# Hybrid decoder layer: issuing background work by per-tile readiness estimates, at finer points

## The chip, the cores and the metric

The kernel runs on one core of a Trainium2 chip. The metric is the device time of one execution in microseconds (us). Before the change three runs took 1051.8, 1048.09 and 1047.04 us; the median is 1048.09 us.

## The reference, cut to what matters

One layer of a decoder on 512 tokens of width 1024: a token-mixing part with two branches, cross-attention into 256 memory tokens, and a mixture of 32 experts. All data are fp32.

```python
h = rms_norm(x, norm_mix_g);  proj = h @ w_in                     # 1024 -> 5120
c_a, c_g, q_r, f_r, i_r, g_r, gate_c, gate_r = split(proj)
# branch 1: u = c_a*sigmoid(c_g); causal depthwise convolution, 31 taps, 512 channels
u = silu(layer_norm(conv(u) + b, ln_g, ln_b));  y_conv = u @ conv_w_out
# branch 2 (HGRN2, 4 heads): decayed scores from cumsum(log f), state per 128 tokens
y_rec = (rms_norm(hgrn2(q_r, f_r, i_r)) * silu(g_r)) @ hgrn_w_out
x = x + (sigmoid(gate_c)*y_conv + sigmoid(gate_r)*y_rec) @ w_mix_out
x = x + cross_attention(rms_norm(x), rms_norm(mem))               # xa_w_q, k, v, o
x = rms_norm(x + moe(rms_norm(x)))     # top group, top 2 of 8 experts in it; 3 matrices each
```

## The kernel before

**Foreground.** The dense products run one after another on TensorE. Each fp32 weight piece of 128 x 1024 is loaded by SyncE into `raw`, rounded to `wh` on ScalarE and the rest `wl = raw - wh` is formed on GpSimd (for the first 16 pieces every second one on VectorE); `push_split` does this (L161 to L171). Each k-step of a product is three matmuls, high x high, high x low and low x high (`mm3`, L226). `gemm_t` (L233) makes transposed outputs, 256 columns at a time in two PSUM banks: one weight piece (`chunk`) serves 24 matmuls, and three pieces are split ahead. `gemm_n` (L261) makes outputs with tokens on partitions. The order of the products is: keys, values (memory); then from `w_in` the HGRN values, f, q, the conv pairs, g, the two gates; then `hgrn_w_out` (`ev_rec`), `conv_w_out` (`ev_conv`), `w_mix_out`, cross-attention, router, experts.

**Background.** Everything else of the mixing part is written as Python generators, "threads": `prepare` (norm of x, transposes, constants), `hgrn_scores` and `hgrn_state` (Ln, scan, seven levels of `z` with Exp on ScalarE and score matmuls `psc` on TensorE, then the states `po`, `pk`, `pst`, then `pot`, `gT`, `oh`, `ol`), `conv` (120 tap instructions on VectorE into two PSUM banks `cva`, then the layer norm: `pmu`, `pvar`, and the split into `chl`). All of this is decided when the program is built: `pump` (L196) is called between groups of foreground matmuls and runs the threads' next steps into the instruction streams. Every engine takes its stream in order, so where a step stands in the stream decides what it holds up.

**The planner.** `Meter` (L43) adds an estimated cost to a clock per engine for each instruction issued. `pump` lifts VectorE's and ScalarE's clocks to TensorE's, then runs a thread while VectorE is less than `SLACK` (3000 ns) ahead of TensorE and the time that the thread last yielded (its due time) has come on TensorE's clock. A bare `yield` is due at once; `now()` is the later of VectorE's and ScalarE's clocks. Before the change an engine's clock does not wait for another engine's results, GpSimd costs nothing, and `gemm_t` calls `pump` twice in each weight piece, after 12 matmuls each. Where a thread's result is needed, `drain` runs the rest of it at once: `drain(t_sc)` at L858 ahead of the `hgrn_w_out` product and `drain()` at L866 ahead of the `conv_w_out` product.

All engine calls go through `Meter.call`, so almost every instruction has line L55; the tile names tell them apart.

**After the mixing part** the expert weights (192 pieces of 1 MB) are loaded into the 16 large buffers of the pool (tag `u`) as these come free, in a fixed order.

Of the kernel before, what the change touches and what calls it, by code (L numbers as in the profile page):

```python
# [19 lines left out]
PSUM = bass.MemoryType.PSUM  # L20
# [8 lines left out]
NH = 4  # L29
# [13 lines left out]
class Meter:  # L43


    def __init__(self, engine, cost):
        self.engine, self.cost, self.clock = engine, cost, 0.0

    def __getattr__(self, name):
        f = getattr(self.engine, name)  # L50

        def call(*args, **kw):
            out = args[0] if args else kw["out"]
            self.clock += self.cost(out, kw)
            return f(*args, **kw)  # L55

        return call
# [10 lines left out]
def act_cost(out, kw):  # L68
    return 200 + 0.72 * free_size(out)


def no_cost(out, kw):
    return 0


def pe_cost(out, kw):
    n = free_size(out)
    if kw.get("lhsT") is not None and kw["lhsT"].dtype == F32R:
        return 0.42 * n if n >= 256 else 213
    return 1.68 * n if kw.get("lhsT") is not None else 110  # L80
# [3 lines left out]
def tile_layer(ctx, tc, x, mem, norm_mix_g, w_in, conv_w, conv_b, conv_ln_g, conv_ln_b, conv_w_out,  # L84
# [5 lines left out]
    meters = [Meter(e, c) for e, c in ((nc.vector, dve_cost), (nc.scalar, act_cost), (nc.gpsimd, no_cost),  # L90
                                       (nc.tensor, pe_cost))]
    V, S, G, PE = meters
# [69 lines left out]
    def push_split(lo_eng=None):  # L162
# [7 lines left out]
        (lo_eng or (V if i < WIDE and i % 2 else G)).tensor_tensor(out=lo, in0=raw, in1=hi.bitcast(F32), op=OP.subtract)  # L170
# [25 lines left out]
    def pump():  # L196
        t0 = meters[3].clock
        for m in meters[:2]:
# [34 lines left out]
    def gemm_t(ncols, nk, act, n, evac, parts=1, mid=None):  # L233
        for c in range(0, ncols, 256):
            pss = [bank("pt") for _ in range(2)]
            ws = []
            for kh in range(nk // 4):
                ws.append(chunk(SPL if parts == 1 else 2))
                for f in range(2):
                    if parts == 1:  # L240
                        for kk in range(4):
                            k = kh * 4 + kk
                            mm3(pss[f][:, :n], [t[:, kk, f * 128:(f + 1) * 128] for t in ws[kh]], act(k),
                                k == 0, k == nk - 1)
                        if kh == nk // 4 - 1:
# [356 lines left out]
    def hgrn_state():  # L602
# [5 lines left out]
        for b in range(NB):  # L608
# [7 lines left out]
            if b < NB - 1:  # L616
# [5 lines left out]
                yield now()  # L622
# [6 lines left out]
                else:  # L629
                    for h in range(NH):  # L630
                        V.scalar_tensor_tensor(hs[:, h, :], hs[:, h, :], elast[:, h * 4 + b:h * 4 + b + 1],
                                               pst[:, h * 128:(h + 1) * 128], op0=OP.mult, op1=OP.add)
            S.copy(out=oN[:, b, :], in_=po)
            yield now()
# [14 lines left out]
        for h in range(NH):  # L649
# [3 lines left out]
            V.scalar_tensor_tensor(gT[:, h, :], ps, vec("on", 0), gT[:, h, :], op0=OP.mult, op1=OP.mult)  # L653
            S.activation(ohl[0][:, h, :], gT[:, h, :], AF.Copy, scale=0.5)
            V.scalar_tensor_tensor(ohl[1][:, h, :], gT[:, h, :], 0.5, ohl[0][:, h, :].bitcast(F32),
                                   op0=OP.mult, op1=OP.subtract)
            yield

    def hgrn_scores():

        S.activation(cum, cum, AF.Ln)
        yield
        ck = u4("ck")
        S.activation(ck, kT, AF.Ln, bias=tiny)
# [5 lines left out]
        ST = u4("ST")  # L670
        state["ST"] = ST
        G.memset(ST, 0.0)

# [47 lines left out]
        for li, m in enumerate(LEVELS):  # L721
# [4 lines left out]
            V.tensor_tensor(out=zv[:, :, 1, :], in0=cv[:, :, 1, :], in1=mid, op=OP.subtract)  # L726
            S.activation(z, z, AF.Exp)
            yield
            if prev is None:
                yield from until("q")  # L730
            else:
                yield from top_scores(prev, 2 * m, at) if li < 3 else scores(li - 1, prev, prev, at)
            V.tensor_tensor(out=zv[:, :, 1, :], in0=zv[:, :, 1, :], in1=qv[:, :, 1, :], op=OP.mult)
            at = now() + (1500 if li else 3000)
# [6 lines left out]
        S.activation(qe, cum, AF.Exp)  # L741
        elast = const.tile([128, 16], F32, name="elast")
# [4 lines left out]
        V.tensor_tensor(out=kevb, in0=cvb[:, :, 127:128].to_broadcast([128, 16, 128]), in1=ckb, op=OP.subtract)  # L747
        S.activation(ke, ke, AF.Exp)
        yield from scores(6, prev, prev, at)
        V.tensor_copy(out=elast, in_=qe.rearrange("p c (n t) -> p (c n) t", t=128)[:, :, 127])  # L750
# [16 lines left out]
    def conv():  # L767
# [9 lines left out]
        for c2 in (0, 2):  # L777
# [12 lines left out]
            if c2 == 0:  # L790
                cv = u4("cv")
                chl.extend((u4("ch", F32R), u4("cl", F32R)))
            for c in (c2, c2 + 1):
# [3 lines left out]
        yield now() + 1000  # L797
        pmu = col_sum(chl, "pmu")
        mu = q4("mu")[:, :512]
        S.activation(mu, pmu, AF.Copy, scale=1.0 / CW)  # L800
        sq = u4("sq")
        for c in range(5):
            if c < 4:
                V.tensor_tensor(out=cv[:, c, :], in0=cv[:, c, :], in1=mu, op=OP.subtract)
# [1040 lines left out]
```

## Time and profile before

| | before |
|---|---|
| median of three runs | 1048.09 us |
| profiled execution, its own time | 1050.78 us |
| its span | 1049.0 us |
| TensorE busy | 965.0 us (92%) |
| VectorE busy | 484.6 us (46%) |
| ScalarE busy | 283.2 us (27%) |
| GpSimd busy | 232.5 us (22%) |
| DMA, read from memory | 258.21 MB, 250 GB/s over the span |

The profile shows one execution. An instruction's row has its start and its duration in us; matmuls are pipelined and their ends are modelled, so two matmuls that follow each other overlap in their rows, and the distance between starts tells what one costs. "Idle before" in square brackets is the time for which the engine stood, and what ended it. PE is TensorE, DVE VectorE, ACT ScalarE, POOL GpSimd. PEclk is the granted share of TensorE's full clock in a stretch.

### The profile page before, as it was taken

The numbers are of one execution on the slowest core, as the hardware profiler recorded it, in microseconds if no ns is written. First come the engines' busy times: TensorE is split into PE (matmuls) and PEld (weight loads), VectorE is DVE, ScalarE is ACT, GpSimd is POOL, SyncE is SP. The second block draws the span as 40 slices with busy tenths as digits, with TensorE's granted clock in tenths as the row PEclk, the third lists the DMA queues.
The fourth block names the chain that finished last, engine by engine and source line by source line (L and its number), as shares of the span: only waits on it lengthen the run. The fifth ranks groups of instructions, "written<-read, shape, count | busy, mean of one in ns | idle before, by whom it ended". The sixth has DMA issues, their size and how long they took to land.

```text
span 1049.0 us, 13180 instructions
## 1 busy us (share of the span) xinstructions
PE 965.0 (92%) x4951; PEld 630.5 (60%) x4951; DVE 484.6 (46%) x967; ACT 283.2 (27%) x461; POOL 232.5 (22%) x122
## 2 busy tenths in 40 slices
PE   7999999998999999999999999999979999776674
PEld 7888778886788888888875444444325543221221
DVE  5581469778985661553335233333303552110113
ACT  5543543432433433354321111111101110000003
POOL 3354321331442575433220000000000000000001
PEclk9999999999999999999999999999989999899988
DMA  9433221111322333212878999999999999999994
GB/s 339 166 87 101 62 80 42 61 61 61 100 87 75 101 108 112 81 61 97 348 283 315 356 371 414 417 417 417 419 416 421 418 417 416 418 417 419 415 397 153
DMA packets 80671, 260.81 MB, mean 249 GB/s; under 512 B 8475, under 2 KB 39356, under 8 KB 59996
## 3 DMA queue, kind: packets, MB, share of 16 engines
q1 hardware_dynamic: 75194, 252.81, 62.4%
q0 software_dynamic: 1728, 3.80, 0.9%
q10 hardware_dynamic: 3682, 3.32, 0.9%
q8 instruction: 40, 0.66, 0.3%
q14 instruction: 27, 0.22, 0.1%
HBM read 258.21 MB, written 4.19 MB: 250 GB/s over the span
## 4 chain that ended last, share of the span: by engine, by line
PE 65%; DMA 23%; issue 4%; DVE 4%; ACT 2%; POOL 1%; SPq 0%; POOLq 0%; DVEq 0%; ACTq 0%
PE pt L55 25%; PE pn L55 12%; PE pg L55 10%; DMA wd<-in_moe_w_down_dram 8%; DMA wg<-in_moe_w_gate_dram 7%; DMA wu<-in_moe_w_up_dram 7%; PE py L55 5%; PE psc L55 3%; PE pc L55 3%; DVE z L55 2%; PE pd L55 1%; PE px L55 1%; PE pot L55 1%; POOL wl L55 1%; PE pw L55 1%
## 5 line engine op out<-in xcount | busy, mean ns | idle before, releaser
L55 POOL TENSOR_TENSOR wl<-raw,wh 128x1024 fp32r<-128x1024 f32 x79 | 195.1, 2474 | 319.0 <-ACT wh L55 303.8
L55 PE MATMUL py<-wd,sghd 128*32 128x512 f32 (+2 forms) x512 | 113.4, 625 | 18.8 <-DMA wd<-in_moe_w_down_dram 18.5
L55 PE MATMUL pt<-hh,wh 128*128 128x512 f32 x288 | 115.6, 401 | 5.0 <-DVE gT L55 3.7
L55 ACT CAST wh<-raw 128x1024 fp32r<-128x1024 f32 x88 | 91.9, 1049 | 100.0 <-PE pt L55 42.5
L55 PE MATMUL pt<-hh,wl 128*128 128x512 f32 x288 | 114.4, 397 | 3.4 <-POOL wl L55 3.4
L55 PE MATMUL pg<-wg,XT 128*32 128x512 f32 (+2 forms) x512 | 103.8, 609 | 14.5 <-DMA wg<-in_moe_w_gate_dram 14.3
L55 PE MATMUL pt<-hl,wh 128*128 128x512 f32 x288 | 114.1, 396 | 0.0
L55 PE MATMUL pg<-wu,XT 128*32 128x512 f32 (+2 forms) x512 | 104.7, 630 | 9.2 <-DMA wu<-in_moe_w_up_dram 9.2
L55 DVE TENSOR_TENSOR xs<-pc,xs 128x512 f32<-128x512 f32 x96 | 58.5, 680 | 88.9 <-PE pc L55 88.9
L55 POOL DMA_INDIRECT X<-xd,idx x12 | 12.1, 1007 | 344.7 <-DVE idx L55 173.6
L55 PEld LDWEIGHTS py<-wd,sghd 128*32 128x32 f32 (+2 forms) x512 | 31.5, 130 | 91.4 <-issue 52.2
L55 DVE SCALAR_TENSOR_TENSOR yl<-py,wsl,yh 128x512 fp32r<-128x512 f32 x26 | 19.4, 750 | 133.4 <-ACT yh L55 132.1
L55 PEld LDWEIGHTS pg<-wg,XT 128*32 128x32 f32 (+2 forms) x512 | 31.3, 129 | 82.7 <-issue 57.6
L55 DVE SCALAR_TENSOR_TENSOR cva<-uT,ca,cva 128x482 f32<-128x482 f32 (+29 forms) x120 | 77.8, 728 | 0.0
L55 PEld LDWEIGHTS pg<-wu,XT 128*32 128x32 f32 (+2 forms) x512 | 30.8, 132 | 75.4 <-issue 53.3
L55 PEld LDWEIGHTS pt<-hh,wh 128*128 128x128 f32 x288 | 55.1, 191 | 17.4 <-DVE gT L55 4.0
L55 PEld LDWEIGHTS pt<-hh,wl 128*128 128x128 f32 x288 | 55.2, 192 | 16.1 <-POOL wl L55 4.3
L55 PEld LDWEIGHTS pt<-hl,wh 128*128 128x128 f32 x288 | 55.3, 192 | 11.3
L55 ACT COPY sghd<-ph 128x512 f32<-128x512 f32 x13 | 7.6, 585 | 161.5 <-PE ph L55 161.5
L55 DVE SCALAR_TENSOR_TENSOR sghd<-pg,wsl,sghd 128x512 f32<-128x512 f32 x13 | 9.8, 750 | 86.3 <-PE pg L55 73.4
L55 ACT ACTIVATE yh<-py,wsl 128x512 fp32r<-128x512 f32 x26 | 17.9, 687 | 114.6 <-PE py L55 114.3
L55 PE MATMUL pt<-h,wh 128*128 128x512 f32 (+1 forms) x160 | 41.5, 348 | 0.0
(324 smaller groups left out, 1563.4 us busy)
## 6 DMA issues: line engine op xcount, KB each, us to landing
wg<-in_moe_w_gate_dram SPq DMA_DIRECT2D x57, 1024.0 KB
wd<-in_moe_w_down_dram SPq DMA_DIRECT2D x56, 1024.0 KB
wu<-in_moe_w_up_dram SPq DMA_DIRECT2D x52, 1024.0 KB
raw<-in_w_in_dram SPq DMA_DIRECT2D x40, 512.0 KB
wu<-in_moe_w_up_dram SPq DMA_DIRECT2D x24, 512.0 KB
wd<-in_moe_w_down_dram SPq DMA_DIRECT2D x16, 512.0 KB
wg<-in_moe_w_gate_dram SPq DMA_DIRECT2D x14, 512.0 KB
raw<-in_xa_w_v_dram SPq DMA_DIRECT2D x4, 1024.0 KB
```

Of the source, the lines that this page charges most:

```text
L55: return f(*args, **kw)
```

## The change

1. **The planner's estimates.** A call now starts at the latest of its engine's clock and the estimated times at which the tiles that it reads are written (`Meter.ready`, by tile, 60 ns after the writer's end). A large all-SBUF `tensor_tensor` on VectorE or GpSimd is put behind an overlapping one of the other engine (`Meter.port`). ScalarE's and TensorE's costs are changed (a matmul of 512 columns from 215 to 227 ns, an fp32 one of 128 columns from 215 to 111 ns, 80 ns for a change of type), GpSimd gets costs, and `pump` lifts its clock too.
2. **Finer points.** `gemm_t` calls `pump` after every three matmuls.
3. **Due times.** In the threads, ScalarE instructions that read a VectorE result are put behind a `yield` of VectorE's clock (before `Exp` of `z`, `ke`, before the splits of the convolution, between `gT` and `oh`), TensorE's steps behind other offsets. `Ln` is cut into eight pieces with a `yield` after each pair, and the clearing of `ST` goes ahead of it.
4. **The convolution's norm** is regrouped: four subtractions first, then squares and splits; the last loop has five rounds in place of six.
5. **Low parts in halves.** GpSimd forms `wl` in two instructions of 512 columns.

No arithmetic is added or removed.

```diff
@@ -43,6 +43,9 @@ class Meter
+    ready, port = {}, []
     def __init__(self, engine, cost):
@@ -51,7 +54,19 @@ Meter.call
             out = args[0] if args else kw["out"]
-            self.clock += self.cost(out, kw)
+            aps = [a for a in list(args) + list(kw.values()) if hasattr(a, "tensor")]
+            t = max([self.clock] + [Meter.ready.get(a.name, 0) for a in aps if a is not out])
+            c = self.cost(out, kw)
+            if name == "tensor_tensor" and c > 300 and all(a.space == SB for a in aps):
+                for t0, t1, e in Meter.port[-4:]:
+                    if e is not self and t0 <= t < t1:
+                        t = t1
+                Meter.port.append((t, t + c, self))
+            self.clock = t + c
+            for a in (out, kw.get("accum_out")):
+                if a is not None:
+                    Meter.ready[a.name] = self.clock + 60
             return f(*args, **kw)
@@ -66,18 +81,20 @@ cost functions
 def act_cost(out, kw):
-    return 200 + 0.72 * free_size(out)
-def no_cost(out, kw):
-    return 0
-def pe_cost(out, kw):
+    return 200 + 0.77 * free_size(out) + (190 if kw.get("accum_out") is not None else 0)
+def pool_cost(out, kw):
+    return 130 + 2.22 * free_size(out)
+def pe_cost(out, kw, last=[None]):
     n = free_size(out)
-    if kw.get("lhsT") is not None and kw["lhsT"].dtype == F32R:
-        return 0.42 * n if n >= 256 else 213
-    return 1.68 * n if kw.get("lhsT") is not None else 110
+    r = kw.get("lhsT") is not None and kw["lhsT"].dtype == F32R
+    c = 80 if r != last[0] else 0
+    last[0] = r
+    return c + (0.4425 * n if r else max(0.87 * n if kw.get("lhsT") is not None else 0, 110))
@@ -87,8 +104,9 @@ tile_layer
     nc = tc.nc
-    meters = [Meter(e, c) for e, c in ((nc.vector, dve_cost), (nc.scalar, act_cost), (nc.gpsimd, no_cost),
+    meters = [Meter(e, c) for e, c in ((nc.vector, dve_cost), (nc.scalar, act_cost), (nc.gpsimd, pool_cost),
                                        (nc.tensor, pe_cost))]
+    Meter.ready, Meter.port = {}, []
     V, S, G, PE = meters
@@ -167,7 +185,10 @@ push_split
         S.copy(out=hi, in_=raw)
-        (lo_eng or (V if i < WIDE and i % 2 else G)).tensor_tensor(out=lo, in0=raw, in1=hi.bitcast(F32), op=OP.subtract)
+        e = lo_eng or (V if i < WIDE and i % 2 else G)
+        for c in (0, 512) if e is G else (0,):
+            sl = slice(c, c + 512 if e is G else 1024)
+            e.tensor_tensor(out=lo[:, sl], in0=raw[:, sl], in1=hi[:, sl].bitcast(F32), op=OP.subtract)
         splits.append(tuple(t.rearrange("p (k c) -> p k c", k=nk) for t in (hi, lo)))
@@ -195,7 +216,7 @@ pump
         t0 = meters[3].clock
-        for m in meters[:2]:
+        for m in meters[:3]:
             m.clock = max(m.clock, t0)
@@ -242,6 +263,8 @@ gemm_t
                                 k == 0, k == nk - 1)
+                            if kk < 3:
+                                pump()
                         if kh == nk // 4 - 1:
@@ -619,7 +642,7 @@ hgrn_state
                 S.copy(out=kn, in_=pk)
-                yield now()
+                yield S.clock + 1500
                 pst = bank("pst")
@@ -630,8 +653,9 @@ hgrn_state
                                                pst[:, h * 128:(h + 1) * 128], op0=OP.mult, op1=OP.add)
+            yield meters[3].clock + 1000
             S.copy(out=oN[:, b, :], in_=po)
-            yield now()
+            yield
             for h in range(NH):
@@ -651,25 +675,27 @@ hgrn_state
             V.scalar_tensor_tensor(gT[:, h, :], ps, vec("on", 0), gT[:, h, :], op0=OP.mult, op1=OP.mult)
+            yield V.clock
             S.activation(ohl[0][:, h, :], gT[:, h, :], AF.Copy, scale=0.5)
...
                                    op0=OP.mult, op1=OP.subtract)
-            yield
+            yield V.clock
-        S.activation(cum, cum, AF.Ln)
-        yield
+        ST = u4("ST")
+        state["ST"] = ST
+        G.memset(ST, 0.0)
         ck = u4("ck")
-        S.activation(ck, kT, AF.Ln, bias=tiny)
+        for h in range(NH):
+            S.activation(cum[:, h, :], cum[:, h, :], AF.Ln)
+            S.activation(ck[:, h, :], kT[:, h, :], AF.Ln, bias=tiny)
+            yield S.clock
         for h in range(NH):
...
         yield
-        ST = u4("ST")
-        state["ST"] = ST
-        G.memset(ST, 0.0)
@@ -724,14 +750,17 @@ hgrn_scores
             V.tensor_tensor(out=zv[:, :, 1, :], in0=cv[:, :, 1, :], in1=mid, op=OP.subtract)
+            yield V.clock
             S.activation(z, z, AF.Exp)
+            ez = S.clock
             yield
...
                 yield from top_scores(prev, 2 * m, at) if li < 3 else scores(li - 1, prev, prev, at)
+            yield ez
             V.tensor_tensor(out=zv[:, :, 1, :], in0=zv[:, :, 1, :], in1=qv[:, :, 1, :], op=OP.mult)
-            at = now() + (1500 if li else 3000)
+            at = V.clock + 2500
             yield
@@ -739,14 +768,17 @@ hgrn_scores
         S.activation(qe, cum, AF.Exp)
+        eq = S.clock
         elast = const.tile([128, 16], F32, name="elast")
...
         V.tensor_tensor(out=kevb, in0=cvb[:, :, 127:128].to_broadcast([128, 16, 128]), in1=ckb, op=OP.subtract)
+        yield V.clock
         S.activation(ke, ke, AF.Exp)
         yield from scores(6, prev, prev, at)
+        yield eq
         V.tensor_copy(out=elast, in_=qe.rearrange("p c (n t) -> p (c n) t", t=128)[:, :, 127])
@@ -790,23 +822,24 @@ conv
                 chl.extend((u4("ch", F32R), u4("cl", F32R)))
+            yield V.clock
             for c in (c2, c2 + 1):
...
                 yield
-        yield now() + 1000
+        yield V.clock + 1000
         pmu = col_sum(chl, "pmu")
+        yield PE.clock + 300
         mu = q4("mu")[:, :512]
...
         sq = u4("sq")
-        for c in range(5):
-            if c < 4:
-                V.tensor_tensor(out=cv[:, c, :], in0=cv[:, c, :], in1=mu, op=OP.subtract)
-                S.activation(sq[:, c, :], cv[:, c, :], AF.Square)
-            if c:
-                split(sq[:, c - 1, :], c - 1)
-            yield
-        yield now() + 4000
+        for c in range(4):
+            V.tensor_tensor(out=cv[:, c, :], in0=cv[:, c, :], in1=mu, op=OP.subtract)
+        for c in range(4):
+            yield Meter.ready[cv.name] - 750 * (3 - c) if c < 3 else V.clock
+            S.activation(sq[:, c, :], cv[:, c, :], AF.Square)
+            split(sq[:, c, :], c)
+        yield V.clock + 500
         pvar = col_sum(chl, "pvar")
@@ -815,18 +848,21 @@ conv
         yield from rsqrt_steps(v, y, t)
-        for c in range(6):
+        for c in range(5):
             if c < 4:
...
                 V.tensor_scalar(cv[:, c, :], cv[:, c, :], hv[:, c:c + 1], hv[:, 4 + c:5 + c], op0=OP.mult, op1=OP.add)
+                w = V.clock
+            if c:
+                V.scalar_tensor_tensor(cv[:, c - 1, :], sq[:, c - 1, :], 1.0, cv[:, c - 1, :], op0=OP.add, op1=OP.mult)
+            yield w
+            if c < 4:
                 S.activation(sq[:, c, :], cv[:, c, :], AF.Tanh)
-            if 0 < c < 5:
-                V.scalar_tensor_tensor(cv[:, c - 1, :], sq[:, c - 1, :], 1.0, cv[:, c - 1, :], op0=OP.add, op1=OP.mult)
+            if c:
+                yield V.clock
                 S.copy(out=chl[0][:, c - 1, :], in_=cv[:, c - 1, :])
-            if c > 1:
-                V.tensor_tensor(out=chl[1][:, c - 2, :], in0=cv[:, c - 2, :], in1=chl[0][:, c - 2, :].bitcast(F32), op=OP.subtract)
-            yield
+                V.tensor_tensor(out=chl[1][:, c - 1, :], in0=cv[:, c - 1, :], in1=chl[0][:, c - 1, :].bitcast(F32), op=OP.subtract)
         dump("cs", cv)
```

## Rows read from the trace of the kernel before

**Rows 1.** Page, part 4: the chain that ended last, shares of the span by engine

```profile
PE 65%; DMA 23%; issue 4%; DVE 4%; ACT 2%; POOL 1%; SPq 0%; POOLq 0%; DVEq 0%; ACTq 0%
```

**Rows 2.** Busy time in stretches: start:end, length, engines' busy us, PEclk, DMA share, GB/s

```profile
25.00:30.00 5.00, 5.00 (x44) 5.00 (x43) 1.99 (x3) 2.09 (x2) 1.23 (x2) 1.00 0.84 318
...
160.00:313.00 153.00, 144.06 (x740) 121.56 (x740) 132.74 (x189) 56.35 (x93) 51.67 (x21) 0.98 0.22 69
500.00:650.00 150.00, 146.87 (x738) 86.88 (x737) 55.41 (x204) 31.71 (x66) 17.50 (x9) 1.00 0.89 345
650.00:1025.00 375.00, 328.33 (x1654) 132.88 (x1653) 105.02 (x258) 34.68 (x54) 8.89 (x9) 0.96 1.02 416
```

**Rows 3.** Waits of TensorE, 10 to 560 us: total us, times, longest us

```profile
PE pt L55 <- DVE gT L55: 3.7, 1, 3.7
PE pt L55 <- POOL wl L55: 3.4, 2, 1.7
...
PE psc L55 <- DVE z L55: 2.7, 3, 1.1
...
PE px L55 <- DVE xn L55: 1.9, 1, 1.9
PE pst L55 <- ACT kn L55: 1.4, 2, 0.7
PE pt L55 <- ACT wh L55: 1.3, 2, 0.8
```

**Rows 4.** First and last of four 5 us stretches with lower PEclk, columns as rows 2

```profile
45.00:50.00 5.00, 4.15 (x15) 3.60 (x16) 4.43 (x5) 1.20 (x3) 0.00 (x0) 0.66 0.00 0
...
275.00:280.00 5.00, 5.00 (x16) 3.97 (x15) 5.00 (x9) 1.05 (x1) 2.42 (x2) 0.67 0.67 209
```

**Rows 5.** Timeline around 125 us, engine by engine: start, us, instruction, [idle before]

```profile
122.13 1.92 ACT L55 ACTIVATE z<-z 128x2048 f32<-128x2048 f32 x1 [6.23 <-DVE z L55]
123.95 1.03 ACT L55 CAST wh<-raw 128x1024 fp32r<-128x1024 f32 x1
...
123.61 0.39 PE L55 MATMUL pt<-hl,wh 128*128 128x512 f32 x1
123.84 0.39 PE L55 MATMUL pt<-hh,wl 128*128 128x512 f32 x1
125.03 0.50 PE L55 MATMUL pt<-hh,wh 128*128 128x512 f32 x1 [0.81 <-ACT wh L55]
...
127.48 0.50 PE L55 MATMUL pt<-hh,wl 128*128 128x512 f32 x1 [1.72 <-POOL wl L55]
```

**Rows 6.** Timeline of VectorE at 42 us and at 250 us

```profile
42.39 3.40 DVE L55 SCALAR_TENSOR_TENSOR xn<-xs,st,gmix 128x1024 f32<-128x1024 f32 x1
...
249.55 0.68 DVE L55 SCALAR_TENSOR_TENSOR gT<-gT,pt 128x512 f32<-128x512 f32 x1
```

**Rows 7.** Timeline of ScalarE: first square of x, Ln and table loads, convolution's splits

```profile
35.28 1.06 ACT L55 ACTIVATE sq<-xs 128x1024 f32<-128x1024 f32 x1
...
109.49 1.28 ACT L55 ACT_TABLE_LOAD   x1
110.79 1.92 ACT L55 ACTIVATE cum<-cum 128x2048 f32<-128x2048 f32 x1
...
267.46 0.59 ACT L55 CAST ch<-cva 128x512 fp32r<-128x512 f32 x1 [3.43 <-DVE cva L55]
```

**Rows 8.** GpSimd's low parts by tile: ns min/median/max, first and last start

```profile
L55 POOL TENSOR_TENSOR ml<-gate,mh x8: 1284/1515/1747, 372.2 to 393.0; 128x512 fp32r<-128x512 f32 x8
...
L55 POOL TENSOR_TENSOR wl<-raw,wh x79: 2355/2397/3440, 13.6 to 536.9; 128x1024 fp32r<-128x1024 f32 x79
```

**Rows 9.** Timeline of VectorE: last write of `ol`, last write of `chl`, last `ev_rec`

```profile
262.14 0.69 DVE L55 SCALAR_TENSOR_TENSOR ol<-gT,oh 128x512 fp32r<-128x512 f32 x1 [0.70 <-ACT oh L55]
...
352.10 1.45 DVE L55 TENSOR_TENSOR cl<-cv,ch 128x512 fp32r<-128x512 f32 x2
...
367.30 0.69 DVE L55 SCALAR_TENSOR_TENSOR gate<-gate,pt 128x512 f32<-128x512 f32 x1 [2.04 <-PE pt L55]
```

More of the change, by code (lines that the diff above doesn't have):

```diff
@@ L19 @@
 AX = mybir.AxisListType
-PSUM = bass.MemoryType.PSUM
+PSUM, SB = bass.MemoryType.PSUM, bass.MemoryType.SB
 SP, ACT, DVE = mybir.EngineType.SP, mybir.EngineType.Activation, mybir.EngineType.DVE
```

## The prediction

> **What bounds the kernel now.** I first read the chain that ended last: it runs through TensorE for 65% of the span, through DMA for 23%, and through the other engines for 7% together [rows 1]. Then the stretches [rows 2]. From 650 to 1025 us the DMA engines are full at 416 GB/s, so there the weights set the pace. From 500 to 650 us they move 345 GB/s: a load starts when a buffer comes free, and TensorE's progress frees it. So the kernel is two parts in series: up to about 560 us TensorE's stream sets the pace, then a stream of weights whose start hangs on that stream. The change touches only the first part. What TensorE gains there comes off the end one for one, unless a new wait takes it; nothing in the second part waits for a fixed time.
>
> TensorE's busy share is no guide to what is left in the first part, since modelled ends hide gaps of a quarter microsecond. Two views tell it. The waits of TensorE [rows 3]: six groups, 14.4 us in 11 waits. And the granted clock: four stretches of 5 us, each right behind a wait for `xn`, `wl`, `gT` or `wl`, stand at 0.66 to 0.67 of the full 2.4 GHz, a mixture of the two levels of 1.2 and 2.4 GHz [rows 4]; the engine stood before each of them and was at full clock up to the wait. A stretch at 0.66 does 3.3 us of work in 5 us, so each costs 1.7 us, 6.7 us in all. A listed wait is also short by the overlap: starts are 0.23 us apart in the undisturbed stream (123.61 to 123.84), and from 123.84 to 125.03 it lost 1.19 - 0.23 = 0.96 us where 0.81 is listed [rows 5]; 0.15 x 11 = 1.7 us more. Sum: 14.4 + 6.7 + 1.7 = 22.8 us. This is the most that a better order can take from TensorE's stream, since its matmuls stay the same.
>
> **Why these waits are there.** At 125 us the order is at fault, not the work. `Exp` of `z` stands on ScalarE for 6.23 us for VectorE's `z`; behind it in the stream stands a rounding `wh`, which starts at 123.95; `wl` follows on GpSimd, and the matmuls stand 0.81 and 1.72 us [rows 5]. At 272 us it is the same with the convolution's split `ch`, which stood 3.43 us for the taps [rows 7]. At 250 us VectorE is late: its `gT` for a product's bank starts at 249.55 and the matmul that needs the bank at 250.29 [rows 3, 6]. At 45 us the product `xn` took 3.40 us on VectorE, beside a low part on GpSimd, and the transposes stood for it [rows 3, 6].
>
> **The change part by part**, each place with its wait, its 0.15 us a time and its clock:
>
> (a) `wh`/`wl` at 125 us: 0.81 + 1.72 + 0.3 + 1.7 = 4.5 us. `yield V.clock` ahead of `Exp` keeps it off ScalarE until VectorE's estimated end. Three pieces are split ahead, each worth 24 x 0.227 = 5.4 us, so a rounding that is late by some microseconds costs nothing: rounding 1.03 us and low part 2.4 us [rows 5, 8] fit into two pieces' 10.9 us with 7 us over. The wait of 6.23 us ate those 7. Estimates may be off by 1 to 2 us here (the scans' cost is untouched), well inside. I take 4.0.
>
> (b) The same at 272 us: 0.5 + 1.7 + 0.3 + 1.7 = 4.2 us; I take 3.8.
>
> (c) `gT` at 250 us: 3.7 + 0.15 + 1.7 = 5.5 us. `yield V.clock` behind `gT` and behind `ol` spreads the four heads' `pot` banks. VectorE may still run up to `SLACK`, 3 us, ahead, and its `scalar_tensor_tensor` taps are not in `Meter.port`. I take 4.3.
>
> (d) `psc` waiting for `z`: 2.7 + 0.45 = 3.2 us. The due time is now 2500 ns behind a clock that knows of `Exp`; I take 2.7.
>
> (e) `pst` waiting for `kn`: 1.4 + 0.3 = 1.7 us. `yield S.clock + 1500` puts at least two groups of three matmuls (0.68 us each) between; I take 1.5.
>
> (f) `xn` at 45 us: 1.9 + 0.15 + 1.7 = 3.7 us. The estimate does not see GpSimd's hold on this form of instruction, but a half low part (1.28 us at the least) can hold it half as long [rows 8], and the three `psc` waits, of 1.1 us at the most, stand in no stretch of lower clock [rows 3, 4]. I take 2.7.
>
> Together 4.0 + 3.8 + 4.3 + 2.7 + 1.5 + 2.7 = 19.0 us.
>
> What it adds. *Halves*: two of 1.28 us against one of 2.40 us, 0.17 us for each of 79 pieces [rows 8], on an engine that is busy 51.67 of 153 us [rows 2]; the first half is there 1.1 us sooner. On the path: 0, and if that cover were gone, 0.17 us for a late piece. *Finer points*: more changes between fp32 and rounded matmuls. No row shows one alone that I trust; from below it is 0, from above I take the 0.15 us of a wait's edge for some ten more groups, 1.5 us; the value 1.0. *Ln in eight pieces*: 512 columns of the nearest form take 0.59 us, so 4 x 0.59 = 2.4 against 1.92 us, twice [rows 7]: 1 us of ScalarE, inside the 7 us above. *Clearing `ST` first*: one GpSimd instruction ahead of a low part, under 2 us, inside the same. *`prepare` earlier*: TensorE's clock now starts at the estimated end of the first split, so the due time of 23000 ns falls near 25 us of the trace where the first square of x stood at 35.28 [rows 7]. The four squares hold ScalarE for 4.2 us (1.06 each) beside the key product, and x must have landed; DMA is still busy at 0.84 from 25 to 30 us [rows 2]. Bounds: 0 if it landed, 4 us if the last block of x had not; I take 1.0, since x is issued before the later value weights. *A step queued behind a new `yield`* costs no engine anything by itself; it can only be late (see the second rival).
>
> Sum: 19.0 - 1.0 - 1.0 = 17.0 us. Against the profiled execution: 1050.8 - 17 = 1033.8 us; that run lies 2.7 us above the median of the three, so 1048.1 - 17 = 1031.1. I say 1031 us.
>
> **A rule that speaks against the change.** After the `Ln` pieces the trace shows a table load of 1.28 us ahead of `Ln` [rows 7], and one more of the same length behind. If a `Tanh` of the q product came between the pieces, each pair would load twice. The Trainium skill, "ScalarE: Activation LUTs" (section "Rules for kernel authors"), says to finish all functions of one table set before switching to another, and cutting `Ln` by `yield`s goes against it. By that rule the sum would lose what three further pairs cost: 3 x 2 x 1.28 = 7.7 us of ScalarE, 0.7 us more than the cover of 7 us, so 1030 to 1032 turns into about 1032 to 1034. I give it little: the first evacuation of the q product comes 48 x 0.227 = 10.9 us after the thread starts, and four pairs due one behind the other take about 6.
>
> **The rivals.** *All of it*: every wait goes and nothing comes, 1048.1 - 22.8 = 1025 us. For it: all six have one cause, order. Against it: VectorE's holds by GpSimd (3.40 us instructions) are only partly in the estimates.
>
> *Slower, the convolution arrives late.* The `conv_w_out` product needs `chl`. Before, its last write ends at 352.10 + 1.45 = 353.55 us, and the product ahead of it ends with the last `ev_rec` at 367.3 [rows 9]: 13.7 us to spare. The change puts some 18 timed `yield`s into this thread, 16 of them in the norm's chain that nothing else fills; each can round up by a pump interval, 0.68 us, and, as I take it, be off by as much again: 18 x 0.68 = 12 us to 25 us. With TensorE 14 us earlier at this point, `drain()` would then hold it. The end moves by what the chain's end E exceeds: it is later than before if E passes 367.3 us, that is if the chain ends 13.7 us later than now, and by over 0.5% beyond 372.5 us. At 22 us later, 375.5, the end is 8 us later, 1056 us. Against it: VectorE is idle for 153 - 132.7 = 20.3 us between 160 and 313 us [rows 2], and taps that fill the waits of the other thread let the chain start up to that much sooner. I expect E near 340. The other deadline is far: `ol` is done at 262.83 us and needed one product of 96 matmuls, 21.8 us, ahead of 367.3, near 345 [rows 9].
>
> *Half*: the estimates put the steps somewhat wrong, so that waits of about 1 us stay in most places, some with their clock: 8 to 12 us are left, 1036 to 1040 us. For it: taps and small column instructions held by GpSimd are not modelled.
>
> *It does not do what it says*: the waits move to other matmuls in the same size, 1043 to 1053 us.
>
> **How the numbers follow.** Forecast, 1027 to 1035 us: 0.45. All of it, 1022 to 1027: 0.18. Half, 1035 to 1042.8: 0.17. No net change: 0.11. Slower: 0.09. The range of 8 in 10 takes the forecast, all but the lowest of the second case and the half case up to 1042: 1023 to 1042 us. A change of 0.5%, 5.2 us, is about what a measurement of this kernel can tell from none. Faster by more: 0.45 + 0.18 + 0.17 = 0.80; within it 0.11; slower by more 0.09.
>
> **What would show it.** In the profile of the changed kernel: the waits of TensorE up to 560 us sum to under 5 us in place of 14.4, and at most one 5 us stretch is below 0.9 of the clock; `Exp` of `z` stands under 2 us for VectorE each time, and no `wh` is late; the first expert load and the stretch of full DMA start 15 to 18 us sooner, and the rate there is still 416 GB/s; the last write of `chl` comes before the last `ev_rec`; there are two table loads around `Ln`. I am wrong if TensorE waits at the start of the `conv_w_out` product, if the squares of x wait for DMA and `wh` behind them is late, or if the first part shortens and the last load does not come sooner.

## The result and the profile after

The changed kernel takes 1038.17 us (median; 1036.33 to 1040.21) where the kernel before, run beside it, takes 1049.22 us: a ratio of 0.9894, 95% interval 0.9861 to 0.9928. It is faster by 11 us; 17 were forecast. The profiled execution took 1040.21 us, its span is 1038.5 us.

**The two parts are still in series.** The chain that ended last, by engine (page, part 4), answers to [rows 1]:

```profile
PE 69%; DMA 21%; DVE 5%; ACT 2%; SPq 2%; issue 1%; ACTq 0%; DVEq 0%
```

The stretches, with the columns of [rows 2], and three of 5 us that answer to [rows 4]:

```profile
160.00:313.00 153.00, 153.00 (x810) 131.08 (x809) 126.07 (x189) 57.79 (x97) 56.57 (x42) 1.00 0.24 73
500.00:650.00 150.00, 146.86 (x746) 82.99 (x746) 53.78 (x200) 27.73 (x54) 16.64 (x14) 1.00 0.91 355
650.00:1025.00 375.00, 331.32 (x1638) 131.62 (x1635) 105.36 (x256) 35.76 (x59) 12.88 (x12) 0.94 0.99 406
...
145.00:150.00 5.00, 2.83 (x14) 2.11 (x15) 3.02 (x3) 3.78 (x5) 2.30 (x2) 0.99 0.29 91
150.00:155.00 5.00, 5.00 (x25) 5.00 (x25) 2.36 (x3) 2.61 (x2) 3.21 (x2) 0.50 0.04 14
155.00:160.00 5.00, 5.00 (x15) 4.13 (x16) 3.90 (x4) 0.00 (x0) 0.00 (x0) 0.50 0.35 105
```

From 160 to 313 us TensorE is now busy throughout, at full clock. The four old stretches of lower clock are gone, but 10 us from 150 to 160 us stand at half, which the kernel before did not have. The full DMA stretch just comes sooner and so ends inside the last row. The first expert load on SyncE's queue went from 494.82 us in the trace of before to this row of after, 10.9 us sooner, and the span is 10.5 us shorter: what the first part gains comes off the end one for one, as forecast.

```profile
483.90 1.87 SPq L1088 DMA_DIRECT2D wg<-in_moe_w_gate_dram  x4
```

**The waits of TensorE**, 10 to 560 us, answer to [rows 3] (total us, times, longest us):

```profile
PE psc L70 <- DVE z L70: 4.4, 3, 2.2
PE pt L70 <- DVE wl L70: 1.9, 2, 1.7
PE pd L70 <- DVE OH L70: 0.9, 2, 0.6
PE px L70 <- DVE xn L70: 0.8, 1, 0.8
PE pt L70 <- ACT ch L70: 0.5, 1, 0.5
PE pn L70 <- DVE wl L70: 0.5, 1, 0.5
PE pt L70 <- DVE cl L70: 0.4, 2, 0.2
```

The groups for `gT`, for GpSimd's `wl`, for `wh` and for `kn` are gone. The pair for `OH` belongs to the expert routing; the kernel before has it too, past 560 us. `psc` waiting for `z` has grown from 2.7 to 4.4 us, and the last of its three waits stands right before the half clock. TensorE's score matmuls in the timeline:

```profile
135.31 2.05 PE L70 MATMUL psc<-z 128*64 128x64 f32 x32 [1.66 <-DVE z L70]
142.86 2.11 PE L70 MATMUL psc<-z 128*32 128x32 f32 x64 [0.52 <-DVE z L70]
149.41 6.66 PE L70 MATMUL psc<-z 128*128 128x64 f32 x32 [2.17 <-DVE z L70]
```

So this place lost 3.2 us before and now loses 4.4 + 3 x 0.15 + 10 x 0.5 = 9.9 us.

**Why `z` is late.** VectorE and ScalarE around 116 us, and `Exp` of the first two levels:

```profile
109.34 0.63 ACT L70 ACTIVATE cum<-cum 128x512 f32<-128x512 f32 x1
...
114.22 0.71 ACT L70 ACTIVATE ck<-kT,tiny 128x512 f32<-128x512 f32 x1
114.95 1.28 ACT L70 ACT_TABLE_LOAD   x1
116.24 0.60 ACT L70 ACTIVATE qT<-pt 128x512 f32<-128x512 f32 x1
...
130.78 1.92 ACT L70 ACTIVATE z<-z 128x2048 f32<-128x2048 f32 x1 [4.66 <-DVE z L70]
139.63 1.92 ACT L70 ACTIVATE z<-z 128x2048 f32<-128x2048 f32 x1 [5.52 <-DVE z L70]
...
116.88 0.69 DVE L70 SCALAR_TENSOR_TENSOR qT<-qT,pt 128x512 f32<-128x512 f32 x1 [8.63 <-ACT qT L70]
117.48 6.67 DVE L70 TENSOR_TENSOR_SCAN cum<-ca,cum 128x512 f32<-128x512 bf16 x4
```

VectorE stands 8.63 us for the first evacuation of the q product, which needs a `Tanh` behind the last `Ln` piece and behind a table load. The four scans are queued behind it. They start at 117.48 us, where they started at 112.74 us in the trace of before, and every level of `z` follows them. They also take 6.67 us where they took 4.57, so the last one ends 6.8 us later, 4.7 by the start and 2.1 by their length. That this place in the order is the cause, and not merely beside it, is what experiments 2, 11 and 12 show.

### The profile page after: what moved, and what is told of

Read it like the earlier page. It is cut to its first block, busy times and chain, and to the rows that moved or that the text cites. A ratio compares the mean times of both kernels' runs of the same rounds, so it can differ in the third digit from the quotient of the medians.

```text
span 1038.5 us, 13293 instructions
## 1 busy us (share of the span) xinstructions
PE 965.6 (93%) x4951; PEld 630.0 (61%) x4951; DVE 479.6 (46%) x967; ACT 284.2 (27%) x467; POOL 255.5 (25%) x201
## 4 chain that ended last, share of the span: by engine, by line
PE 69%; DMA 21%; DVE 5%; ACT 2%; SPq 2%; issue 1%; ACTq 0%; DVEq 0%
PE pt L70 24%; PE pg L70 12%; PE pn L70 12%; DMA wg<-in_moe_w_gate_dram 7%; DMA wd<-in_moe_w_down_dram 6%; PE py L70 5%; DMA wu<-in_moe_w_up_dram 5%; PE psc L70 3%; PE pc L70 3%; DMA raw<-in_xa_w_v_dram 2%; PE pd L70 2%; DVE z L70 1%; PE pot L70 1%; PE px L70 1%; PE pw L70 1%; DVE cum L70 1%
## 5 line engine op out<-in xcount | busy, mean ns | idle before, releaser
L70 POOL TENSOR_TENSOR wl<-raw,wh 128x512 fp32r<-128x512 f32 x158 | 219.1, 1409 | 288.3 <-ACT wh L70 288.0
L70 PE MATMUL py<-wd,sghd 128*32 128x512 f32 (+2 forms) x512 | 115.5, 645 | 18.8 <-DMA wd<-in_moe_w_down_dram 18.6
L70 ACT CAST wh<-raw 128x1024 fp32r<-128x1024 f32 x88 | 92.0, 1050 | 125.8 <-PE pt L70 75.3
L70 PE MATMUL pg<-wg,XT 128*32 128x512 f32 (+2 forms) x512 | 106.3, 624 | 12.4 <-DMA wg<-in_moe_w_gate_dram 12.2
L70 PEld LDWEIGHTS pt<-hl,wh 128*128 128x128 f32 x288 | 54.7, 190 | 10.9
L70 PEld LDWEIGHTS pt<-hh,wh 128*128 128x128 f32 x288 | 54.7, 190 | 10.9
```

## The experiments

Each is timed beside the kernel before (1049.5 to 1050.4 us); "the change" is the changed kernel, 1038.17 us.

**1. The scan's cost.** The planner counts 698 ns for a scan; the trace shows 6.67 / 4 = 1.67 us.

```diff
             c = self.cost(out, kw)
+            if name == "tensor_tensor_scan" and c > 300:
+                c = 1650
```

> The changed kernel with one estimate corrected: a scan of 512 columns counts 1650 ns on VectorE's clock in place of 698. Theory (the scans' estimate): in the changed kernel the four scans took 6.67 us where the planner counted 2.8, so z was late, three psc groups stood 4.4 us and the clock stood at half for 10 us (5 us lost). With the estimate corrected the psc waits fall under 1 us in all, no stretch between 130 and 170 us is below 0.9 of the clock, the first part is 8 to 10 us shorter up to 170 us; at the end 4 to 9 us are left of it, about 1029 to 1034 us, as the convolution's norm already ends with the product ahead of conv_w_out and takes some back. Rival (GpSimd's hold on VectorE's z instructions, not the scan): the psc waits stay above 3 us and the time within 2 us of 1038.

Measured: 1041.38 us, ratio 0.9924 (0.99 to 0.9948). The longest of its waits of TensorE:

```profile
PE pmu L72 <- ACT ch L72: 2.4, 2, 1.8
PE pt L72 <- ACT ch L72: 1.7, 2, 1.5
PE pmu L72 <- DVE cl L72: 1.0, 1, 1.0
```

All waits for `z` and the half clock at 150 us are gone, and yet nothing is gained: now the convolution's column sums `pmu` and the start of `conv_w_out` wait, with lower clock from 307 to 317 and from 355 to 362 us. The last tap ends no later than in the change (300.76 against 302.22 us), but the column sums start 4.9 us earlier (303.83 against 308.75 us), ahead of the last split. Why a truer cost leads to that order was not separated. The theory was right on the place and wrong on the time.

**2. Ln whole.**

```diff
-        for h in range(NH):
-            S.activation(cum[:, h, :], cum[:, h, :], AF.Ln)
-            S.activation(ck[:, h, :], kT[:, h, :], AF.Ln, bias=tiny)
-            yield S.clock
+        S.activation(cum, cum, AF.Ln)
+        S.activation(ck, kT, AF.Ln, bias=tiny)
+        yield S.clock
```

> The changed kernel with Ln in two whole instructions of 2048 columns again, as before, with one yield behind them. Theory (the scans' estimate): the scans start 2 to 4 us sooner (after the first Ln, not after the fourth pair and a q evacuation), which makes up for most of their wrong estimate: psc waits fall by 2 us or more, and the time falls by 2 to 7 us, 1031 to 1036 us. Rival (Ln pieces keep ScalarE free for the foreground): a wh is late behind the whole Ln, TensorE stands for wh or wl, and the time rises by 2 us or more.

Measured: 1030.01 us, ratio 0.9808 (0.9769 to 0.9847): 8.2 us better than the change, from three lines. The scans start at 111.51 us, `psc` waits 0.5 us in all, and no 2.5 us stretch between 8 and 556 us is below full clock. The pieces were costed at nothing in the prediction.

**3. Low parts whole again**, the rest as in the change (one instruction of 1024 in place of two of 512).

> The changed kernel with GpSimd's low parts whole again (79 instructions of 1024 columns). If the halves matter, VectorE's two-input instructions beside them are held up to 2.2 us instead of 1.1, TensorE's waits up to 560 us rise from about 9 us by 3 us or more, and the time rises by 3 to 8 us, 1041 to 1046 us. Rival (the order alone did it): within 2 us of 1038.

Measured: 1039.96 us (0.9866 to 0.9945), 1.8 us more than with halves. The 3 to 8 us that I expected did not come, and 1.8 us is within the spread (1038.64 to 1042.42 us here, 1036.33 to 1040.21 with halves). The waits for `z` grow from 4.4 to 6.7 us, the longest to 2.9.

**4. No finer points**, the rest as in the change (the two added lines of `gemm_t` taken out).

> The changed kernel without the pump calls after every three matmuls: two per weight piece, as before, 2.7 us apart. Theory (each timed yield rounds up to the next pump call): the norm of the convolution, 55.8 us from the last tap to the last write of chl in the changed kernel, takes 75 us or more, chl is late by 15 us or more and TensorE stands ahead of the conv_w_out product; the time is 1050 us or more, no better than before. Rival (the order and the estimates bring the gain, the fine points little): TensorE's waits stay within 3 us of the changed kernel's and the time within 4 us of 1038.

Measured: 1044.09 us (0.9918 to 0.9962), not the 1050 us or more of my theory. No wait for `z`, but the convolution's steps come late; the first two groups:

```profile
PE pt L70 <- ACT ch L70: 7.7, 3, 5.2
PE pt L70 <- ACT wh L70: 2.1, 1, 2.1
```

The last low part of `chl` is written at 361.6 + 0.7 = 362.3 us, 4.2 us later than with finer points. The outcome of the prediction's second rival, a late `chl`, exists; its size here is 7.7 us of wait and about 7 us of clock, from 350 to 365 us. Its mechanism does not show: from the last tap to the last write it is 48.3 us, less than the 55.8 of the change. What is late is the last tap, which ends at 314.03 us in place of 302.22.

Here `Tanh`s of the q product did fall between the `Ln` pieces, with six table loads around `Ln` where the change has two. Two of the six, and the scans:

```profile
113.89 1.28 ACT L70 ACT_TABLE_LOAD   x1
115.18 0.63 ACT L70 ACTIVATE cum<-cum 128x512 f32<-128x512 f32 x1
...
116.44 1.28 ACT L70 ACT_TABLE_LOAD   x1
...
118.97 5.62 DVE L70 TENSOR_TENSOR_SCAN cum<-ca,cum 128x512 f32<-128x512 bf16 x4
```

The scans start 1.5 us later than in the change, behind two evacuations, and no score group waits for `z`: the first one starts at 137.64 us, behind 24 more of the products' matmuls than in the change. Experiment 1 shows the same with scans at 116.46 us and the first score group at 136.64 us, behind 18 more. So in these orders late scans cost TensorE something only where its score groups stand early.

**5 to 7. One part alone**, put into the kernel before: the estimates (`Meter.call`, the costs, `pump` over three meters), the finer points, the halves.

> The kernel before, with the new estimates of Meter alone (start of a call at the estimated end of what it reads, new costs, GpSimd's clock lifted too); no finer points, no new due times, no halves, old norm. If the estimates alone carry the gain (the better order follows from them), the waits of TensorE up to 560 us fall from 14.4 to about 6 us and the time is 1036 to 1041 us. My theory is that the estimates pay only with the due times that use them, since a bare yield is due at once whatever the clock says: the waits stay at 10 to 18 us and the time is 1044 to 1053 us.

> The kernel before, with a pump after every three matmuls of gemm_t and nothing else. If the finer points alone carry the gain: 1036 to 1041 us, since a step is taken up at most 0.7 us after it is due in place of 2.7 us. My theory: VectorE's steps come in smaller portions, so VectorE and ScalarE stand less, but the order that holds wh at 125 and 272 us (Exp of z, split of the convolution ahead of it on ScalarE) stays: at least those two waits with their clock (8.7 us by the prediction's steps) stay and the time is 1042 to 1052 us. Slower than 1053 would say that steps taken up more eagerly hold the weight roundings more often.

> The kernel before, with the low parts on GpSimd in halves and nothing else. In the changed kernel the halves were worth 1.8 us (1039.96 without, 1038.17 with). If that is their own price: 1046 to 1049 us. GpSimd's hold on VectorE's xn at 42 us falls from 3.4 us to about 2.3 us and the wait for xn (1.9 us with 1.7 us of clock) shrinks or goes; the wait for wl at 127 us falls by about 1.1 us. If the order is so delicate that any change of it counts, anything within 1040 to 1055 us.

Measured: estimates 1037.24 us (0.9855 to 0.9936), finer points 1044.25 us (0.9937 to 0.997), halves 1043.37 us (0.9926 to 0.9961). My theory on the estimates fell: with no new due time they gain 12.3 us, as much as the whole change. The waits with the estimates alone:

```profile
PE pt L70 <- DVE cl L70: 4.7, 1, 4.7
PE pt L70 <- DVE wl L70: 2.2, 2, 1.6
PE px L70 <- DVE xn L70: 1.3, 1, 1.3
PE pd L70 <- DVE OH L70: 0.9, 2, 0.6
PE psc L70 <- DVE z L70: 0.8, 1, 0.8
PE pt L70 <- POOL wl L70: 0.5, 1, 0.5
```

`Exp` of `z` still stands there for VectorE, 7.32 and 6.03 us at the first two levels, and no `wh` is late behind it. The finer points alone clear the places at 250 and 272 us and the waits for `kn` too, but not the one at 125 us (0.82 and 1.72 us of wait). `Ln` is whole in both other kernels, and `z` is late in them as well, by 3.1 us with the finer points and 2.1 us with the halves, each followed by lower clock. The halves are worth 6.1 us alone, against 1.8 us in the change, which is not clear of noise: a price in one order need not hold in another.

**8. The old norm**: the kernel of experiment 2 with the convolution's norm, from the column sums on, in the form of before (bare yields, six rounds).

> The changed kernel with Ln whole (1030.01 us), and with the convolution's norm, from the first column sums on, in the form of the kernel before: bare yields in place of timed ones, six rounds in place of five, subtractions and squares in one loop. If the timed yields make the norm 12 us longer, as the comparison of the two traces says (55.8 us from the last tap to the last low part against 43.4 us), the norm takes 42 to 46 us here and chl is written 8 to 14 us sooner than in the kernel with Ln whole. Since chl is only 1 us late there, and the bare yields put ScalarE's squares ahead of VectorE's results again and so in front of a weight rounding, I expect new waits of 0 to 4 us with or without lower clock: 1028 to 1034 us. If the regrouped norm is what keeps the end of the first part free of waits, it is 1034 to 1040 us.

Measured: 1032.38 us (0.9807 to 0.9888), within 2.4 us of the new norm. The expected shorter norm did not come. The last low part of the taps and the last of `chl` on VectorE, here:

```profile
299.91 0.69 DVE L70 TENSOR_TENSOR cl<-cva,ch 128x512 fp32r<-128x512 f32 x1 [1.14 <-ACT ch L70]
...
348.41 1.17 DVE L70 TENSOR_TENSOR cl<-cv,ch 128x512 fp32r<-128x512 f32 x1
```

with the estimates alone:

```profile
303.43 0.69 DVE L70 TENSOR_TENSOR cl<-cva,ch 128x512 fp32r<-128x512 f32 x1 [1.14 <-ACT ch L70]
...
352.59 1.46 DVE L70 TENSOR_TENSOR cl<-cv,ch 128x512 fp32r<-128x512 f32 x2
```

and in the change:

```profile
308.65 0.69 DVE L70 TENSOR_TENSOR cl<-cva,ch 128x512 fp32r<-128x512 f32 x1 [1.14 <-ACT ch L70]
...
357.36 0.69 DVE L70 TENSOR_TENSOR cl<-cv,ch 128x512 fp32r<-128x512 f32 x1 [0.68 <-ACT ch L70]
```

From the end of the one to the end of the other: 49.0, 49.9 and 48.7 us. In the kernel before the first of them was at 312.68 us, so with [rows 9] it was 353.55 - 313.37 = 40.2 us, and with the finer points alone it is 342.95 - 305.18 = 37.8 us. In these three kernels with the estimates the norm is some 9 us longer, with timed yields or without; in experiment 4 it is 5.5 us longer. That a clock which includes waits lets the thread go on less often would explain it, but no run tests this.

**9 and 10. Parts together**: estimates and halves; then estimates, halves and finer points, which is the change without its due times, its Ln pieces and its norm.

> The kernel before with the estimates and the halves of the low parts, nothing else. Alone they gained 12.3 and 6.1 us. If both gains add: about 1031 us. If they take the same waits (the low part at 127 us, z, xn): 1034 to 1038 us. The convolution's low part, 4.7 us late at the start of conv_w_out with the estimates alone, is in neither; if it stays, 1034 or more.

> The kernel before with the estimates, the halves and the finer points: the change without its due times, without Ln in pieces and without the regrouped norm. If the due times are what the estimates need, as my prediction had it: 1036 to 1042 us. If the estimates set the order by themselves (since pump lets no thread go on while VectorE's clock is ahead, and that clock now knows of ScalarE's results), the due times add nothing: 1028 to 1033 us, as with Ln whole and all due times (1030.0 us).

Measured: 1032.99 us (0.9794 to 0.9874) and 1032.02 us (0.9787 to 0.9867). The gains of estimates and halves nearly add (12.3 + 6.1 = 18.4 against 17.4), and the finer points add 1, which is within the spread. What is left is one place, the convolution's low part; the first row of the latter's waits:

```profile
PE pt L70 <- DVE cl L70: 3.4, 2, 2.6
```

The due times and the regrouped norm are worth 2 to 3 us more, if `Ln`'s own is left out: on the same chip this kernel ran at 1031.2 to 1032.9 us, that of experiment 11 at 1027.6 to 1030.2.

**11. Eight pieces, no yield between them.**

```diff
         for h in range(NH):
             S.activation(cum[:, h, :], cum[:, h, :], AF.Ln)
+        for h in range(NH):
             S.activation(ck[:, h, :], kT[:, h, :], AF.Ln, bias=tiny)
-            yield S.clock
+        yield S.clock
```

> The changed kernel with Ln still cut in eight instructions, but the eight issued one behind the other (all of cum, then all of ck) with one yield behind them. Tells the cut from the yields between the pieces. Theory: the price of the eight pieces is the order, since the yields put a weight rounding between them and the scans behind the first qT evacuation; cutting alone costs ScalarE about 1 us (8 x 0.62 to 0.71 against 1.92 + 1.99 us), and the first scan can start after the first piece. Then the scans start at 110 to 113 us, and the time is that of Ln whole within 2 us: 1028.5 to 1032.5 us. Rival: the number of instructions and the extra 1 us of ScalarE put the later steps wrong: 1035 to 1040 us.

Measured: 1029.34 us (0.9756 to 0.9838), level with experiment 2. Cutting alone costs nothing that shows; the eight take 2.20 + 2.55 = 4.75 us of ScalarE, and the first scan starts at 110.08 us, behind the first piece.

**12. Eight pieces, bare yields**: the change with `yield` in place of `yield S.clock` behind each pair, one word.

> The changed kernel with its Ln in eight alternating pieces and four yields, but the yields bare (due at once) in place of due at ScalarE's clock. On VectorE its stream is then the one of the kernel with no yields between the pieces: the scans ahead of the first qT evacuation, where the changed kernel has that one instruction ahead of them. If the position of this one instruction is the price: scans start at 110 to 113 us, 1028 to 1032 us. If alternating the two forms of Ln is the price: the scans start 1 to 2 us later, z waits return, 1033 to 1038 us.

Measured: 1029.71 us (0.977 to 0.9844). The instruction streams of this kernel and of the change are the same on TensorE, GpSimd and SyncE. They differ in the place of one rounding `wh` on ScalarE and of one instruction on VectorE (+ is the change):

```
 TENSOR_SCALAR cum<-cum,ca 128x512
+SCALAR_TENSOR_TENSOR qT<-qT,pt 128x512
 SCAN cum<-ca,cum 128x512 x4
 TENSOR_TENSOR ck<-cum,ck 128x2048
-SCALAR_TENSOR_TENSOR qT<-qT,pt 128x512 x2
+SCALAR_TENSOR_TENSOR qT<-qT,pt 128x512
```

In its timeline the scans start 8 us sooner than in the change, and the third group of score matmuls waits 0.16 us and takes 3.79 us where it took 6.66:

```profile
109.44 5.07 DVE L70 TENSOR_TENSOR_SCAN cum<-ca,cum 128x512 f32<-128x512 bf16 x4 [1.75 <-ACT cum L70]
114.62 3.26 DVE L70 TENSOR_TENSOR ck<-cum,ck 128x2048 f32<-128x2048 f32 x1
117.80 1.27 DVE L70 SCALAR_TENSOR_TENSOR qT<-qT,pt 128x512 f32<-128x512 f32 x2
...
144.55 3.79 PE L70 MATMUL psc<-z 128*128 128x64 f32 x32 [0.16 <-DVE z L70]
```

So the place of two instructions is worth 8.5 us by the medians, and 9.75 us between the two profiled executions that the rows are from (1040.21 and 1030.46 us). It is the score groups' loss: 9.9 us in the change, under 0.5 us here. Of the two instructions it is the evacuation that holds the scans: the first piece that they read is ready at 109.34 + 0.63 = 109.97 us in the change, so the moved rounding does not.

## Why the prediction was right or wrong

**The number.** 1038.17 us is inside the stated range, 1023 to 1042 us, and outside the forecast's own 1027 to 1035 us. It stands where the case *Half* stood, 1036 to 1040 us, but not by its mechanism: that case had waits of about 1 us left in most places, while here most places cleared and one grew. That it fell in the range is in part luck.

**Right: the frame.** A gain in the first part comes off the end one for one, and 22.8 us was a fair size of the loss: the `conv_w_out` product starts at 367.10 us in the trace of before, at 354.01 us in the change and at 344.30 us in experiment 12, 13.1 and 22.8 us sooner. The equal figure is chance: experiment 12 still has some 2 us of waits ahead of that product, so 22.8 us was not quite the most. The forecast of 17 us is not far from the gain of nearly this change, 19.9 us with one word less, though that gain does not come by the due times.

**Right in size: (a), (b), (c), (e).** Their waits and their clock are gone: 4.5 + 4.2 + 5.5 + 1.7 = 15.9 us back, where I took 13.6. But the reason that I gave is refuted: in (a) and (b) I ascribed it to the `yield V.clock` ahead of ScalarE's steps. Without these yields, experiment 5 loses 0.5 us there (GpSimd's `wl` at 129 us) and experiment 10 nothing, and neither waits at the old 250 and 272 us or for `kn`. At 125 us it is the estimates, and which of their three parts was not separated; at the other places the estimates alone or the finer points alone are enough. A sign that I had listed, `Exp` of `z` standing under 2 us, failed (4.66 and 5.52 us) and means nothing: in experiment 12 it stands 5.53 us, and no `wh` is late. An engine that stands costs only what is queued behind it.

**Right: (f).** The wait for `xn` fell from 1.9 to 0.8 us and its clock returned: 3.7 - 0.95 = 2.75 us, 2.7 taken. The `prepare` thread, now earlier, was a smaller loss than the 1.0 that I took: the first square of x starts at 27.79 us, and the one wait behind its steps on VectorE is 0.50 us for `wl`, in the value product.

**Wrong: (d), by way of the Ln pieces.** I took a gain of 2.7 us and costed the eight pieces as "1 us of ScalarE, inside the 7 us above", that is, at nothing. (d) lost 6.7 us more than before. What failed is the counting of a cut as busy time only. The `yield S.clock` behind each pair made the thread due later than the q product's first evacuation; VectorE takes its stream in order, so it stood 8.63 us and the scans behind it. I had even worked out when that evacuation comes, 10.9 us after the thread starts against about 6 for the pieces, to dismiss the table loads, and did not ask what lands ahead of the scans on VectorE if the pieces come a little later. The table loads themselves were as I said, two. The rule of the Trainium skill, "ScalarE: Activation LUTs", section "Rules for kernel authors", to do all of one table set before switching, had no occasion in the change: no `Tanh` fell between the pieces. In experiment 4 it had one, four loads of 1.28 us more, and TensorE waited for nothing between 39.8 and 297.9 us. 2.7 + 6.7 = 9.4 us is more than the whole miss of 6 us. Three listed signs failed with it: the waits up to 560 us sum to 9.4 us where I had said under 5, two stretches of 5 us stand at 0.50, and the first expert load came 10.9 us sooner, not 15 to 18.

**Half right: the convolution.** The rival's lateness came, at 2 us in place of its 8 or more. `chl` ends at 358.05 us, where I expected about 340: the last tap ends 8 us sooner than before, not up to 20, and from there to the last write it is 55.8 us in place of 43.0 (the last tap of before ends at 310.56 us; what I expected of experiment 8 has 43.4). I put the difference, 12.8 us, down to the rounding of 18 timed yields; experiment 8 shows that 8 to 9 us of them come with the estimates and remain with bare yields. The other 4.3 lie between the last tap and the last split (7.1 us against 2.8). There VectorE stands for a step of the other thread that got ahead of the splits:

```profile
304.90 1.36 DVE L70 SCALAR_TENSOR_TENSOR ol<-gT,oh 128x512 fp32r<-128x512 f32 x1 [2.68 <-ACT oh L70]
```

The kernels with a timed yield there have 2.5 to 9.3 us, those without it 2.5 to 4.2, so the yield alone does not set it. TensorE did wait in the `conv_w_out` product, the sign that I had named for being wrong: 0.22 + 0.52 + 0.22 us. From its start to that of `w_mix_out` it takes 23.72 us where it took 21.76, so 2 us are lost there.

**Sum.** 15.9 + 2.75 - 6.7 - 2 = 10 us, and a new wait for `wl` in the key product, 1.75 us at 20 us, takes some 1.9: 8 of the 10.9 us measured; the 0.50 us in the value product takes it to 7.4. The starts of the products tell where the other 3.5 lie. From the first product of f to `hgrn_w_out` it is 247.73 us in place of 259.04, 2.1 us better than 15.9 - 6.7; the waits for `po` (0.5 us before, none after) are part of that. The key product is 1.1 us longer, not 1.9, since in the trace of before its matmuls came 0.21 us apart up to 12 us, where they come 0.12 us apart in the change. The rest is spread.

## What to carry to other kernels

When background steps are woven into in-order queues by estimates, read for every yield which instruction of another thread can now get ahead of the next one on each engine, and what that one waits for: one early evacuation in front of a scan was worth 8.5 us, while cutting an operation in eight cost nothing that shows. Then ask where the consumer stands: in experiment 4 two such evacuations cost nothing at that place, since the score matmuls came later. Look first at the planner's clock; here the estimates and the halved low parts carried 17.4 of some 20 us. But a truer figure alone is no gain: the scan's true cost gave 1041.38 us against 1038.17. And price a part in the order that it will stand in: the halves were worth 6.1 us in one and 1.8 us, not clear of noise, in another.

## What the runs showed of the hardware

A wait's length alone did not tell here what clock followed. In the trace of the change, 1.75 us in the key product and 1.66 us ahead of the first score group were followed by full clock and 2.17 us by 10 us at half; in the trace of before 1.72 us was followed by a lower stretch of 5 us [rows 4, 5], as was 3.7 us. At half clock the same 32 score matmuls took 6.66 us in place of 3.79.

A scan of 128 x 512 took 4.57 / 4 = 1.14 us in the trace of before and 6.67 / 4 = 1.67 us in the change, beside halves on GpSimd, which in turn took 4.09 us for two in place of 2.53:

```profile
113.86 2.53 POOL L70 TENSOR_TENSOR wl<-raw,wh 128x512 fp32r<-128x512 f32 x2 [1.47 <-ACT wh L70]
118.97 4.09 POOL L70 TENSOR_TENSOR wl<-raw,wh 128x512 fp32r<-128x512 f32 x2 [2.58 <-ACT wh L70]
```

In the trace of before no low part ran on GpSimd during the scans. Small column instructions on VectorE take longer too. In the trace of experiment 11, beside the same kind of halves (2.55 and 2.54 us for two):

```profile
13.00 0.36 DVE L70 TENSOR_SCALAR st<-st 128x2 f32<-128x2 f32 x2
13.39 1.49 DVE L70 TENSOR_TENSOR st<-st 128x2 f32<-128x2 f32 x2
16.96 2.56 DVE L70 TENSOR_SCALAR tmp<-ident,st 128x128 f32<-128x128 f32 x2
```

In experiment 12, where the halves start 0.4 us after the pair that writes `tmp`, that pair takes 0.48 us in place of 2.56, and the wait in the key product is 0.36 us in place of 1.75. No run tries these two by themselves.
